# Decoder block on one core: gate columns inside the first head's value projection, keys turned by full-precision transposes, a 128-row bias product

## The chip, the cores and the metric

One core of a Trainium2 chip runs the whole block: one sequence of 1024 positions, 1024 channels, in float32. The metric is the device time of one execution in microseconds, as the median of several runs; less is better. Engines are called as in the profile: PE is TensorE, PEld its weight loads, DVE is VectorE, ACT is ScalarE, POOL is GpSimd, SP issues most DMAs.

## What is computed

```python
h = rms_norm(x, norm_mix_g) * (1.0 + sc1) + sh1
proj = h @ w_in + b_in
glu_in, qk_in, v, o_pre, if_pre, merge_pre = jnp.split(proj, IN_SPLITS, axis=-1)
...
qk = silu(causal_depthwise_conv(qk_in, qk_conv_w, qk_conv_b))
q, k = jnp.split(qk, 2, axis=-1)
...
gates = jnp.moveaxis(if_pre, -1, 1)
hm = mlstm_chunkwise(heads(q), heads(k) * (MLSTM_HEAD_DIM ** -0.5), heads(v),
                     gates[:, :MLSTM_HEADS], gates[:, MLSTM_HEADS:])
```

There are 4 heads of 256 channels. `if_pre` is 8 columns wide: an input gate and a forget gate for each head. In the recurrence the state is updated by `C = decay * C + sum_s w_s k_s v_s^T`, in which `w` comes from the gates. A convolution branch (31 taps, on the GLU of the first 2048 columns of `proj`), merge gates, an output projection and a SwiGLU FFN stand around it.

## The kernel before

Every large product is made in three parts for accuracy: each operand is split into a rounded part (hi) and the rest (lo), both in the type fp32r, and hi*hi, hi*lo and lo*hi are summed in PSUM. `hh` and `hl` hold h in that way, channels on the partitions, 8 tiles of 128 x 1024. `load_split` (L143) loads weights of 8 x 128 rows and 128 columns, ACT rounds them into `whi`, DVE subtracts to `wlo`. `wblock` (L370) makes one 128-column block of `proj` from them, 48 products of 512 columns at L159.

The stretch from about 70 to 830 us is the mixers. After two GLU tiles (`glu`, L394), the loop at L730 takes the heads in turn. For each head `qkv` (L516) makes two key tiles and two query tiles (`qk_tile`, L496: `wblock`, a 4-tap convolution on DVE, Silu on ACT, the split), then the values: `v_weights` loads 1024 x 256 weights in two halves, and `v_half` (L543) takes four tiles of 128 positions each: one bias product with `ones_v` (64 rows, two of them not zero: the bias's hi and lo at rows 0 and 32; L549), and 24 products of 256 columns (L552 to L554). ACT and DVE empty the sum into `vh` and `vl` (L559, L560).

For the first head `gates` (L412) runs in between: a generator whose steps `mix` (L383) interleaves with those of `qkv`. It loads the 8 gate columns into `wif_raw`, puts hi and lo beside each other into the first 16 of 128 weight columns (`wif`, the rest zero), makes 32 products of 512 columns (L423), copies the 16 x 1024 result to SBUF and turns it back by eight transposes with 16 rows (L432). Then come a chain of short DVE instructions, scans along the sequence, and the tables `iw`, `wsc`, `en`, `dec`, `Mc`.

`mlstm` (L593) works in four chunks of 256 positions. For three of them the keys must be turned to have positions on the partitions: L621 multiplies the key's hi and lo by `shift_id`, an identity beside zeros, four products of 256 columns for each 128 positions. The result is scaled by `wsc` into `kwh`, `kwl` (L624, L625). `mlstm` is mixed with filler blocks (GLU tiles, merge gates, output gates).

The convolution taps (L340, DVE, 128 x 1024 each) go through a list `bg`: `pump` (L82) emits some after each block with a later priority. The order on each engine is not the order of the code: a scheduler places every instruction by priority and by its own model of time. Each engine then works in that order and waits on semaphores. Buffers matter around the change: weights have two each of `wraw`, `whi`, `wlo`; the tag `t4` has three of 128 x 1024 (the sigmoids of the GLU tiles use them); PSUM has two accumulators `mm` of two banks.

Of the kernel before, what the change touches and what calls it, by code (L numbers as in the profile page):

```python
# [17 lines left out]
KT = 8  # L18
# [31 lines left out]
def hybrid_block(ctx: ExitStack, tc: tile.TileContext, x, c, w_ada, b_ada, norm_mix_g, w_in, b_in,  # L50
# [49 lines left out]
    ones_v = const.tile([64, 128], F32R, name="ones_v")  # L100
# [223 lines left out]
    shift_id = hp.tile([128, 2, 256], F32R, name="shift_id")  # L324
    nc.gpsimd.memset(shift_id.bitcast(F32), 0.0)
    nc.vector.tensor_copy(shift_id[:, 0, 0:128], ident)
    nc.vector.tensor_copy(shift_id[:, 1, 128:256], ident)
# [83 lines left out]

    def gates():  # L412
        wif_raw = hp.tile([128, KT, 8], F32, name="wif_raw")
        nc.sync.dma_start(wif_raw, win[:, IF0:IF0 + 8].rearrange("(k p) e -> p k e", p=128))
        wif = wp.tile([128, KT, 128], F32R, name="wif", tag="whi")
        nc.gpsimd.memset(wif.bitcast(F32), 0.0)
        nc.vector.tensor_copy(wif[:, :, 0:8], wif_raw)
        nc.vector.tensor_sub(wif[:, :, 8:16], wif_raw, wif[:, :, 0:8].bitcast(F32))
        acc = ps_mm()
        for k in range(KT):  # L420
            for i, rhs in enumerate((hh, hl)):
                for h in range(2):
                    nc.tensor.matmul(acc[:, h, :], wif[:, k, :], rhs[k][:, h * 512:(h + 1) * 512],  # L423
                                     start=(k == 0 and i == 0), stop=(k == KT - 1 and i == 1))
        ifT = tmp4()
        nc.scalar.activation(ifT, flat(acc), AF.Copy)
        yield

        yield
        pg = ps_a()  # L430
        for b in range(8):
            nc.tensor.transpose(pg[:, b * 16:(b + 1) * 16], ifT[0:16, b * 128:(b + 1) * 128], ident[0:16, 0:16])  # L432
        pgv = pg[:, 0:128].rearrange("p (b j) -> p b j", j=16)
        gsum = hp.tile([128, 8, 8], F32, name="gsum")
        nc.vector.tensor_add(gsum, pgv[:, :, 0:8], bif[:, None, :].to_broadcast([128, 8, 8]))
        nc.vector.tensor_add(gsum, gsum, pgv[:, :, 8:16])
# [56 lines left out]
        for t, sgn in ((iw, 1.0), (wsc, 1.0), (en, -1.0), (dec, 1.0)):  # L493
            nc.scalar.activation(t, t, AF.Exp, scale=sgn)

    def qk_tile(col0, conv_i, scale, name):  # L496
# [9 lines left out]
        nc.scalar.activation(cv, cv, AF.Silu, bias=cols["qk_b"][:, conv_i:conv_i + 1])  # L506
# [3 lines left out]
        if scale == 1.0:  # L510
            nc.vector.tensor_sub(lo, cv, hi.bitcast(F32))
        else:
            nc.vector.scalar_tensor_tensor(lo, cv, scale, hi.bitcast(F32), op0=OP.mult, op1=OP.subtract)
        return hi, lo

    def qkv(h):  # L516
# [7 lines left out]
        b_raw, b_hi, b_two = (hp.tile([64, 256], dt, name=n) for n, dt in (("vb_raw", F32), ("vb_hi", F32R), ("vb_two", F32R)))  # L524
        nc.gpsimd.memset(b_raw, 0.0)
        for r in (0, 32):
            nc.sync.dma_start(b_raw[r:r + 1, :], b_in[0:1, bcols])
# [4 lines left out]
        def v_weights():  # L532
            ws = []
            for kh in range(2):
                raw, hi, lo = (wp.tile([128, KT, 128], dt, name=n, tag=n).rearrange("p (k a) e -> p k (a e)", a=2)
                               for n, dt in (("wraw", F32), ("whi", F32R), ("wlo", F32R)))
                nc.sync.dma_start(raw, win[kh * 512:(kh + 1) * 512, bcols].rearrange("(k p) e -> p k e", p=128))
                nc.scalar.activation(hi, raw, AF.Copy)
                nc.vector.tensor_sub(lo, raw, hi.bitcast(F32))
                ws.append((hi, lo))  # L540
            return ws
# [735 lines left out]
```

## Time and profile before

| | us |
|---|---|
| median of 3 runs | 1760.76 (1760.38 to 1761.39) |
| span of the profiled execution, first to last instruction | 1757.5 |
| PE busy | 1716.9 (98%) |
| DVE busy | 1253.3 (71%) |
| ACT busy | 610.9 (35%) |
| POOL busy | 72.9 (4%) |

The time of a run and the span of the profiled execution differ by what lies around the first and the last instruction. Busy time is the time in which at least one instruction of the engine is under way; PE's products overlap, so a group's mean duration is longer than the distance from one start to the next.

### The profile page before, as it was taken

To read this page: it belongs to the slowest core of one execution; us is meant where nothing else is said; L and a number is where in the kernel's file an instruction comes from. 1 tells how busy PE (TensorE), PEld (TensorE's weight loads), DVE (VectorE), ACT (ScalarE), POOL (GpSimd) and SP (SyncE) were. 2 spreads that over 40 slices of the span, in tenths; PEclk is the share of its full clock that TensorE was granted. 3 is DMA by queue.
4 is the path that set the end of the run, shared out by engine and by line. 5 is a ranking of instruction groups with operands and counts; after the bars stand their busy time and mean duration, and the time that the engine had idled before them with its cause. 6 is when DMAs were issued, how large, how long until landed. Compare 5 with 4: busy or idle time off the path is not lost.

```text
span 1757.5 us, 21022 instructions
## 1 busy us (share of the span) xinstructions
PE 1716.9 (98%) x8448; PEld 1436.9 (82%) x8448; DVE 1253.3 (71%) x1652; ACT 610.9 (35%) x791; POOL 72.9 (4%) x121
## 2 busy tenths in 40 slices
PE   5999999999999999999999999999999999999998
PEld 4788888888888888888888788888888888878887
DVE  6888998996689858737689567866666665685243
ACT  6434334322533243223522366423222321232122
POOL 3100001000100000000000000000000000000000
PEclk8999999999999999999999999999999999999999
DMA  9121111111111211224497643322222222653221
GB/s 333 33 60 40 46 60 49 49 60 60 49 37 60 62 46 48 73 60 163 136 374 261 204 156 109 108 84 72 84 84 84 72 85 90 221 168 104 64 89 56
DMA packets 194712, 179.93 MB, mean 102 GB/s; under 512 B 7463, under 2 KB 166711, under 8 KB 194615
## 3 DMA queue, kind: packets, MB, share of 16 engines
q1 hardware_dynamic: 177367, 146.61, 26.8%
q10 hardware_dynamic: 17248, 31.99, 5.0%
q8 instruction: 66, 1.08, 0.3%
q14 instruction: 31, 0.25, 0.0%
HBM read 146.06 MB, written 32.51 MB: 102 GB/s over the span
## 4 chain that ended last, share of the span: by engine, by line
PE 90%; DVE 4%; DMA 3%; issue 1%; ACT 1%; POOL 0%; SPq 0%; POOLq 0%; DVEq 0%; ACTq 0%
PE mm L159 39%; PE mm L1054 5%; PE mm L1055 5%; PE mm L1056 4%; PE mm L552 2%; PE mm L1240 2%; PE mm L1239 2%; PE mm L1241 2%; PE mm L553 2%; PE mm L554 2%; PE pc L1054 1%; DVE macc L268 1%; PE pc L1056 1%; PE pc L1055 1%; PE pa L1056 1%
## 5 line engine op out<-in xcount | busy, mean ns | idle before, releaser
L340 DVE SCALAR_TENSOR_TENSOR cacc<-a,col,cacc 128x1024 f32<-128x1024 f32 x240 | 307.3, 1286 | 4.1 <-ACT cacc L338 1.4
L159 PE MATMUL mm<-hh,whi 128*128 128x512 f32 x864 | 272.8, 392 | 0.8 <-ACT t L364 0.8
L159 PE MATMUL mm<-hl,whi 128*128 128x512 f32 x864 | 271.0, 392 | 0.0
L159 PE MATMUL mm<-hh,wlo 128*128 128x512 f32 x864 | 270.6, 391 | 0.0
L159 PEld LDWEIGHTS mm<-hh,whi 128*128 128x128 f32 x864 | 161.1, 188 | 32.8 <-ACT t L364 1.2
L159 PEld LDWEIGHTS mm<-hh,wlo 128*128 128x128 f32 x864 | 161.3, 188 | 32.3
L159 PEld LDWEIGHTS mm<-hl,whi 128*128 128x128 f32 x864 | 160.5, 188 | 30.9 <-issue 0.2
L149 ACT ACTIVATE whi<-wraw 128x1024 fp32r<-128x1024 f32 x62 | 65.8, 1062 | 228.7 <-PE mm L159 178.5
L150 DVE TENSOR_TENSOR wlo<-wraw,whi 128x1024 fp32r<-128x1024 f32 x60 | 73.2, 1220 | 26.1 <-ACT whi L149 26.0
L552 PE MATMUL mm<-whi,hh 128*128 128x256 f32 x256 | 76.2, 298 | 0.0
L1054 PE MATMUL mm<-Bh,gh 128*128 128x512 f32 (+1 forms) x192 | 71.6, 375 | 1.5 <-ACT gh L994 1.0
L553 PE MATMUL mm<-whi,hl 128*128 128x256 f32 x256 | 72.5, 283 | 0.0
L1055 PE MATMUL mm<-Bl,gh 128*128 128x512 f32 (+1 forms) x192 | 71.5, 373 | 0.6 <-DVE Bl L976 0.6
L554 PE MATMUL mm<-wlo,hh 128*128 128x256 f32 x256 | 71.8, 283 | 0.0
L1056 PE MATMUL mm<-Bh,gl 128*128 128x512 f32 (+1 forms) x192 | 71.2, 372 | 0.0
L505 DVE SCALAR_TENSOR_TENSOR cacc<-qkraw,col,cacc 128x1024 f32<-128x1024 f32 x48 | 61.5, 1280 | 6.7 <-ACT cacc L503 6.0
L1243 DVE TENSOR_TENSOR x<-x,mm 128x1024 f32<-128x1024 f32 x24 | 29.3, 1219 | 51.1 <-PE mm L1241 47.0
L1119 ACT ACTIVATE whi<-wraw 128x512 fp32r<-128x512 f32 (+2 forms) x32 | 25.3, 790 | 110.6 <-PE mm L1241 72.9
L552 PEld LDWEIGHTS mm<-whi,hh 128*128 128x128 f32 x256 | 48.8, 191 | 4.1
L1240 PE MATMUL mm<-fa,wlo 128*128 128x512 f32 x128 | 50.1, 392 | 1.0 <-DVE wlo L1120 0.9
L1239 PE MATMUL mm<-fa,whi 128*128 128x512 f32 x128 | 50.0, 390 | 0.9 <-DVE cu L1082 0.9
L1241 PE MATMUL mm<-fa,whi 128*128 128x512 f32 x128 | 49.9, 390 | 0.0
(442 smaller groups left out, 3898.0 us busy)
## 6 DMA issues: line engine op xcount, KB each, us to landing
wraw<-in_w_in_dram SPq DMA_DIRECT2D x64, 512.0 KB, 4.2
awt<-in_w_ada_dram SPq DMA_DIRECT2D x32, 512.0 KB, 8.1
graw<-in_w_ffn_up_dram SPq DMA_DIRECT2D x24, 512.0 KB, 3.8
uraw<-in_w_ffn_up_dram SPq DMA_DIRECT2D x22, 512.0 KB, 4.7
draw<-in_w_ffn_down_dram SPq DMA_DIRECT2D x22, 512.0 KB, 4.4
act_d<-cg ACTq DMA_DIRECT2D x38, 256.0 KB, 2.2
wad<-in_w_ada_dram SPq DMA_DIRECT2D x16, 512.0 KB, 10.2
wraw<-in_w_out_dram SPq DMA_DIRECT2D x16, 512.0 KB, 4.3
```

Of the source, the lines that this page charges most:

```text
L150: (eng or nc.vector).tensor_sub(lo, raw, hi.bitcast(F32))
L159: nc.tensor.matmul(flat(acc)[:, a:b], lhs[:, k, :], rhs[k][:, a:b], start=(first and k == 0), stop=(last and k == kt - 1))
L340: nc.vector.scalar_tensor_tensor(acc, a[:, j:j + S], dw_col(j, ct), acc, op0=OP.mult, op1=OP.add)
L552: nc.tensor.matmul(o, hh[k][:, ts_], hi[:, k % 4, :], start=False, stop=False)
L553: nc.tensor.matmul(o, hl[k][:, ts_], hi[:, k % 4, :], start=False, stop=False)
L554: nc.tensor.matmul(o, hh[k][:, ts_], lo[:, k % 4, :], start=False, stop=(k == KT - 1))
L1054: nc.tensor.matmul(o, a, rh, start=(k == 0), stop=False)
L1055: nc.tensor.matmul(o, a, rl, start=False, stop=False)
L1056: nc.tensor.matmul(o, b, rh, start=False, stop=(k == 3))
L1239: nc.tensor.matmul(o, hi[:, i, :], his[i][:, a:b], start=(i == 0), stop=False)
L1240: nc.tensor.matmul(o, lo[:, i, :], his[i][:, a:b], start=False, stop=False)
L1241: nc.tensor.matmul(o, hi[:, i, :], los[i][:, a:b], start=False, stop=(i == nf - 1))
```

## The change

It has three parts. The gate columns no longer have products of their own: in the first head's value projection the rounded weights get 16 more columns (8 hi, 8 lo), and DVE sums them out of PSUM into `gsum`. For that the wide weights (272 columns a row tile) lie in the three `t4` buffers, an accumulator holds two tiles of positions in place of four, and the values of each head are a generator of their own (`v_part`), which runs ahead of keys and queries for the first head and behind them for the others. The bias product has 128 rows, with more zeros. And the keys are turned by transposes of a full-precision copy `kf` (the first 768 positions, the three chunks that need it); the factor 1/16 of the keys goes into `wsc`.

```diff
-    ones_v = const.tile([64, 128], F32R, name="ones_v")
+    ones_v = const.tile([128, 128], F32R, name="ones_v")
...
-    shift_id = hp.tile([128, 2, 256], F32R, name="shift_id")
-    nc.gpsimd.memset(shift_id.bitcast(F32), 0.0)
-    nc.vector.tensor_copy(shift_id[:, 0, 0:128], ident)
-    nc.vector.tensor_copy(shift_id[:, 1, 128:256], ident)
...
+    gsum = hp.tile([128, 8, 8], F32, name="gsum")
+    wif_raw = hp.tile([128, KT, 8], F32, name="wif_raw")
+    nc.sync.dma_start(wif_raw, win[:, IF0:IF0 + 8].rearrange("(k p) e -> p k e", p=128))
+
     def gates():
-        wif = wp.tile([128, KT, 128], F32R, name="wif", tag="whi")
...
-        nc.vector.tensor_copy(wif[:, :, 0:8], wif_raw)
-        nc.vector.tensor_sub(wif[:, :, 8:16], wif_raw, wif[:, :, 0:8].bitcast(F32))
-        acc = ps_mm()
-        for k in range(KT):
-            for i, rhs in enumerate((hh, hl)):
-                for h in range(2):
-                    nc.tensor.matmul(acc[:, h, :], wif[:, k, :], rhs[k][:, h * 512:(h + 1) * 512],
-                                     start=(k == 0 and i == 0), stop=(k == KT - 1 and i == 1))
-        ifT = tmp4()
-        nc.scalar.activation(ifT, flat(acc), AF.Copy)
...
-        pg = ps_a()
-        for b in range(8):
-            nc.tensor.transpose(pg[:, b * 16:(b + 1) * 16], ifT[0:16, b * 128:(b + 1) * 128], ident[0:16, 0:16])
...
-        nc.vector.tensor_add(gsum, pgv[:, :, 0:8], bif[:, None, :].to_broadcast([128, 8, 8]))
-        nc.vector.tensor_add(gsum, gsum, pgv[:, :, 8:16])
         gview = gsum.rearrange("p (c s) j -> p s c j", s=2)
         nc.vector.tensor_copy(gi, gview[:, :, :, 0:4])
...
             nc.scalar.activation(t, t, AF.Exp, scale=sgn)
+        nc.vector.tensor_scalar(wsc, wsc, 1.0 / 16, None, op0=OP.mult)
...
-        nc.scalar.activation(cv, cv, AF.Silu, bias=cols["qk_b"][:, conv_i:conv_i + 1])
+        bias = cols["qk_b"][:, conv_i:conv_i + 1]
+        if name == "k":
+            kf = hp.tile([128, 768], F32, name=f"kf{conv_i % 2}")
+            nc.scalar.activation(kf, cv[:, 0:768], AF.Silu, bias=bias)
+            nc.scalar.activation(cv[:, 768:S], cv[:, 768:S], AF.Silu, bias=bias)
+            hi, lo = (hp.tile([128, S], F32R, name="k" + n, tag="k" + n, bufs=2) for n in "hl")
+            for src, a, b in ((kf, 0, 768), (cv[:, 768:S], 768, S)):
+                nc.scalar.activation(hi[:, a:b], src, AF.Copy, scale=scale)
+                nc.vector.scalar_tensor_tensor(lo[:, a:b], src, scale, hi[:, a:b].bitcast(F32), op0=OP.mult, op1=OP.subtract)
+            return hi, lo, kf
+        nc.scalar.activation(cv, cv, AF.Silu, bias=bias)
...
-    def qkv(h):
+    def v_part(h):
...
-        b_raw, b_hi, b_two = (hp.tile([64, 256], dt, name=n) for n, dt in (("vb_raw", F32), ("vb_hi", F32R), ("vb_two", F32R)))
+        b_raw, b_hi, b_two = (hp.tile([128, 272], dt, name=n) for n, dt in (("vb_raw", F32), ("vb_hi", F32R), ("vb_two", F32R)))
...
+        his, los = [], []
+        if h == 0:
+            wide = [ha.tile([128, S], F32R, name="t4", tag="t4", bufs=3)[:, 0:816].rearrange("p (k e) -> p k e", e=272) for _ in range(3)]
+            his = [wide[k // 3][:, k % 3] for k in range(KT)]
+            for i, t in enumerate(wide):
+                n = min(3, KT - 3 * i)
+                ks = slice(3 * i, 3 * i + n)
+                nc.vector.tensor_copy(t[:, 0:n, 256:264], wif_raw[:, ks])
+                nc.vector.tensor_sub(t[:, 0:n, 264:272], wif_raw[:, ks], t[:, 0:n, 256:264].bitcast(F32))
+        for kh in range(2):
+            raw, hi, lo = (wp.tile([128, KT, 128], dt, name=n, tag=n).rearrange("p (k a) e -> p k (a e)", a=2)
+                           if n != "whi" or h else None for n, dt in (("wraw", F32), ("whi", F32R), ("wlo", F32R)))
+            nc.sync.dma_start(raw, win[kh * 512:(kh + 1) * 512, bcols].rearrange("(k p) e -> p k e", p=128))
...
+                his += [hi[:, k] for k in range(4)]
+            else:
+                for t, a, k0, k1 in (((wide[0], 0, 0, 3), (wide[1], 0, 3, 4)), ((wide[1], 1, 0, 2), (wide[2], 0, 2, 4)))[kh]:
+                    o = t[:, a:a + k1 - k0, 0:256]
+                    nc.scalar.activation(o, raw[:, k0:k1], AF.Copy)
+                    nc.vector.tensor_sub(lo[:, k0:k1], raw[:, k0:k1], o.bitcast(F32))
+            los += [lo[:, k] for k in range(4)]
...
+        for g in range(8 // n):
             acc = ps_mm()
-            for i in range(4):
-                t = g * 4 + i
+            for i in range(n):
+                t = g * n + i
...
-                o = acc[:, i // 2, (i % 2) * 256:(i % 2) * 256 + 256]
-                nc.tensor.matmul(o, ones_v, b_two, start=True, stop=False)
+                o = acc[:, i // 2, (i % 2) * 256:(i % 2) * 256 + 256] if h else acc[:, i, 0:272]
+                nc.tensor.matmul(o, ones_v, b_two[:, 0:w], start=True, stop=False)
                 for k in range(KT):
-                    hi, lo = ws[k // 4]
-                    nc.tensor.matmul(o, hh[k][:, ts_], hi[:, k % 4, :], start=False, stop=False)
-                    nc.tensor.matmul(o, hl[k][:, ts_], hi[:, k % 4, :], start=False, stop=False)
-                    nc.tensor.matmul(o, hh[k][:, ts_], lo[:, k % 4, :], start=False, stop=(k == KT - 1))
+                    nc.tensor.matmul(o, hh[k][:, ts_], his[k], start=False, stop=False)
+                    nc.tensor.matmul(o[:, 0:256], hh[k][:, ts_], los[k], start=False, stop=False)
+                    nc.tensor.matmul(o, hl[k][:, ts_], his[k], start=False, stop=(k == KT - 1))
                 pump(PUMP / 4)
                 yield
...
-
+            if h == 0:
+                gs = gsum[:, 2 * g:2 * g + 2]
+                nc.vector.tensor_add(gs, acc[:, :, 256:264], bif[:, None, :].to_broadcast([128, 2, 8]))
+                nc.vector.tensor_add(gs, gs, acc[:, :, 264:272])
+        return vh, vl
+
+    def qk_part(h):
         q, k = [], []
...
-        ws = v_weights()
-        for g in range(2):
-            yield from v_half(g, ws)
-        return q, k, vh, vl
+        return q, k
...
                     for j in range(2):
-                        for i in range(2):
-                            nc.tensor.matmul(o, k[j][i][:, ks], shift_id[:, j, :], start=(j == 0 and i == 0),
-                                             stop=(j == 1 and i == 1))
+                        nc.tensor.transpose(o[:, j * 128:(j + 1) * 128], k[j][2][:, ks], ident)
                     w = wsc[:, s, c, h:h + 1]
...
         if h == 0:
-            qkv0 = returned(qkv(0), box)
-            mix(gates(), qkv0, GM)
-            run(qkv0)
+            qk0 = returned(qk_part(0), box)
+            run(returned(v_part(0), vbox))
+            mix(gates(), qk0, GM)
+            run(qk0)
         else:
-            run(returned(qkv(h), box))
+            run(returned(qk_part(h), box))
+            run(returned(v_part(h), vbox))
```

The scheduler orders the instructions anew. On PE, the place behind the second GLU tile (`mm` is the accumulator in PSUM, `whi`, `wlo` the weights, `hh`, `hl` the block's input) read before:

```order
L159 MATMUL mm_635<-hl7_460,whi_631 128x512 x2
L159 MATMUL mm_635<-hh7_89,wlo_632 128x512 x2
L423 MATMUL mm_707<-hh0_82,wif_703 128x512 x2
L423 MATMUL mm_707<-hl0_314,wif_703 128x512 x2
L423 MATMUL mm_707<-hh1_83,wif_703 128x512 x2
L423 MATMUL mm_707<-hl1_317,wif_703 128x512 x2
```

Now the value projection of the first head stands there, and takes its first four products of the first accumulator and of the second before it comes to the weights in the third buffer (`t4_716`):

```order
L551 MATMUL mm_794<-wlo_731,hh4_86 128x256
L552 MATMUL mm_794<-t4_715,hl4_407 128x272
L550 MATMUL mm_794<-t4_715,hh5_87 128x272
L551 MATMUL mm_794<-wlo_731,hh5_87 128x256
L552 MATMUL mm_794<-t4_715,hl5_410 128x272
L550 MATMUL mm_737<-t4_716,hh6_88 128x272
L551 MATMUL mm_737<-wlo_731,hh6_88 128x256
L552 MATMUL mm_737<-t4_716,hl6_457 128x272
```

The 32 products of L423 are gone, and 38 products stand between the GLU tile and the first one that reads `t4_716`.

On DVE, at the same place (`a` is the second GLU tile's product, `cacc` the conv taps, `wlo` the low part of the v weights, `gsum` the gate sums):

```order
L341 SCALAR_TENSOR_TENSOR a_685<-mm_631,col5_513,t4_625 128x1024
L537 TENSOR_TENSOR wlo_731<-wraw_730,t4_715 128x512
L336 SCALAR_TENSOR_TENSOR cacc_577<-a_563,col3_517,cacc_577 128x1024
L523 CAST t4_716<-wif_raw_698 128x2x8
L537 TENSOR_TENSOR wlo_731<-wraw_730,t4_716 128x512
L336 SCALAR_TENSOR_TENSOR cacc_577<-a_563,col3_517,cacc_577 128x1024
L524 TENSOR_TENSOR t4_716<-wif_raw_698,t4_716 128x2x8
L336 SCALAR_TENSOR_TENSOR cacc_577<-a_563,col4_521,cacc_577 128x1024 x4
L558 TENSOR_TENSOR vl_701<-mm_737,vh_700 128x2x256
L561 TENSOR_TENSOR gsum_697<-mm_737,bif_403 128x16
L336 SCALAR_TENSOR_TENSOR cacc_577<-a_563,col4_521,cacc_577 128x1024
L562 TENSOR_TENSOR gsum_697<-gsum_697,mm_737 128x16
```

Before, `a` was followed by one low part of a key's weights and then by taps; now the split of the third weight tile and the emptying of the accumulators stand between the taps.

In the first chunk of the first head, PE's list around the turned keys (`pa`, `pn` are PSUM, `vh`, `sch` the values and the scores) changes in this way:

```order
-L621 MATMUL pa_1440<-shift_id_537,kh_838 128x256
-L621 MATMUL pa_1440<-shift_id_537,kl_839 128x256
-L621 MATMUL pa_1440<-shift_id_537,kh_939 128x256
-L621 MATMUL pa_1440<-shift_id_537,kl_940 128x256
-L573 MATMUL pn_1469<-vh_742,sch_1427 128x258
+L621 MATMUL pa_1420<-ident_69,kf0_1063 128x128
+L621 MATMUL pa_1420<-ident_69,kf1_1178 128x128
+L574 MATMUL pn_1445<-vh_700,sch_1407 128x258
```

Four products become two transposes, at the same place between the filler's products and the first product with the scores; there are 24 such places.

## Rows read from the trace of the kernel before

**Rows 1.** The page, busy time, share of the span and instructions of each engine.
```profile
PE 1716.9 (98%) x8448; PEld 1436.9 (82%) x8448; DVE 1253.3 (71%) x1652; ACT 610.9 (35%) x791; POOL 72.9 (4%) x121
```

**Rows 2.** Busy time by stretch: length, then each engine, clock, DMA share, GB/s.
```profile
core 0: us, PE busy (x) PEld busy (x) DVE busy (x) ACT busy (x) POOL busy (x), PEclk, DMA share, GB/s
90.00:140.00 50.00, 50.00 (x228) 41.13 (x227) 44.97 (x61) 19.49 (x20) 0.42 (x4) 1.00 0.22 64
...
170.00:330.00 160.00, 160.00 (x883) 138.12 (x882) 144.53 (x180) 57.67 (x70) 12.70 (x22) 1.00 0.19 53
...
650.00:830.00 180.00, 180.00 (x968) 154.26 (x967) 118.73 (x161) 56.06 (x68) 6.40 (x13) 1.00 0.26 82
990.00:1000.00 10.00, 6.46 (x22) 4.93 (x21) 7.31 (x10) 3.69 (x4) 0.00 (x0) 0.83 0.63 197
```

**Rows 3.** Timeline of PE around a bias product: start, duration, line, operands, count.
```profile
148.12 0.28 PE L554 MATMUL mm<-wlo,hh 128*128 128x256 f32 x1
148.32 0.38 PE L549 MATMUL mm<-vb_two,ones_v 64*128 64x256 f32 x1
148.63 0.39 PE L552 MATMUL mm<-whi,hh 128*128 128x256 f32 x1
148.86 0.28 PE L553 MATMUL mm<-whi,hl 128*128 128x256 f32 x1
```

**Rows 4.** Groups of PE by form: count, busy time, mean duration.
```profile
L621 PE MATMUL pa<-shift_id,kh 128*128 128x256 f32 x48 | 12.4, 280 | 0.0
L549 PE MATMUL mm<-vb_two,ones_v 64*128 64x256 f32 x32 | 12.2, 380 | 0.0
```

**Rows 5.** Timeline of PE around the gates' eight small transposes.
```profile
104.74 0.61 PE L159 MATMUL mm<-hh,wlo 128*128 128x512 f32 x2
105.29 0.67 PE L432 MATMUL pa<-ident,t 16*128 16x16 f32 x8
105.89 0.74 PE L159 MATMUL mm<-hh,whi 128*128 128x512 f32 x2
106.47 0.63 PE L159 MATMUL mm<-hl,whi 128*128 128x512 f32 x2
```

**Rows 6.** Timeline of PE, first of the gates' products and first one after them.
```profile
89.78 0.62 PE L423 MATMUL mm<-hh,wif 128*128 128x512 f32 x2
...
97.04 0.62 PE L159 MATMUL mm<-hh,whi 128*128 128x512 f32 x2
```

**Rows 7.** Timeline of PE around one group of turned keys.
```profile
202.31 0.28 PE L621 MATMUL pa<-shift_id,kh 128*128 128x256 f32 x1
...
202.79 0.28 PE L573 MATMUL pn<-vh,sch 128*128 128x258 f32 x1
202.91 0.28 PE L574 MATMUL pn<-vl,sch 128*128 128x258 f32 x1
```

**Rows 8.** Timeline of PE around two transposes of the decay mask.
```profile
175.36 0.62 PE L159 MATMUL mm<-hh,whi 128*128 128x512 f32 x2
175.82 0.38 PE L582 MATMUL pa<-ident,Mc 128*128 128x128 f32 x2
...
176.50 0.62 PE L159 MATMUL mm<-hh,wlo 128*128 128x512 f32 x2
```

**Rows 9.** The page, DMA issues: count, KB each, median us to landing.
```profile
wraw<-in_w_in_dram SPq DMA_DIRECT2D x64, 512.0 KB, 4.2
```

**Rows 10.** Timeline of DVE before and at the end of the second GLU tile.
```profile
80.09 0.19 DVE L417 CAST wif<-wif_raw 128x64 fp32r<-128x64 f32 x1
...
81.55 7.88 DVE L340 SCALAR_TENSOR_TENSOR cacc<-a,col,cacc 128x1024 f32<-128x1024 f32 x6
90.05 1.28 DVE L345 SCALAR_TENSOR_TENSOR a<-mm,col,t 128x1024 f32<-128x1024 f32 x1 [0.62 <-PE mm L159]
91.25 1.22 DVE L150 TENSOR_TENSOR wlo<-wraw,whi 128x1024 fp32r<-128x1024 f32 x1
```

**Rows 11.** Waits of PE: what was waited for, in total, times, longest.
```profile
PE pa L946 <- ACT whi L940: 3.5, 1, 3.5
```

More of the change, by code (lines that the diff above doesn't have):

```diff
@@ L509, in qk_tile @@
         nc.scalar.activation(hi, cv, AF.Copy, scale=scale)
[L510 to L513, printed above, removed]
+        nc.vector.tensor_sub(lo, cv, hi.bitcast(F32))
         return hi, lo
-    def qkv(h):
+    def v_part(h):
         vh = hp.tile([128, 8, 258], F32R, name="vh")
@@ L523, in qkv @@
         bcols = slice(V0 + h * 256, V0 + h * 256 + 256)
-        b_raw, b_hi, b_two = (hp.tile([64, 256], dt, name=n) for n, dt in (("vb_raw", F32), ("vb_hi", F32R), ("vb_two", F32R)))
+        b_raw, b_hi, b_two = (hp.tile([128, 272], dt, name=n) for n, dt in (("vb_raw", F32), ("vb_hi", F32R), ("vb_two", F32R)))
         nc.gpsimd.memset(b_raw, 0.0)
         for r in (0, 32):
-            nc.sync.dma_start(b_raw[r:r + 1, :], b_in[0:1, bcols])
+            nc.sync.dma_start(b_raw[r:r + 1, 0:256], b_in[0:1, bcols])
         nc.scalar.activation(b_hi, b_raw, AF.Copy)
@@ L530, in qkv @@
         nc.vector.tensor_sub(b_two[32:64, :], b_raw[32:64, :], b_hi[32:64, :].bitcast(F32))
[L532 to L537, printed above, removed]
+        his, los = [], []
@@ L538, in v_weights @@
+        for kh in range(2):
+            raw, hi, lo = (wp.tile([128, KT, 128], dt, name=n, tag=n).rearrange("p (k a) e -> p k (a e)", a=2)
+                           if n != "whi" or h else None for n, dt in (("wraw", F32), ("whi", F32R), ("wlo", F32R)))
+            nc.sync.dma_start(raw, win[kh * 512:(kh + 1) * 512, bcols].rearrange("(k p) e -> p k e", p=128))
+            if h:
                 nc.scalar.activation(hi, raw, AF.Copy)
                 nc.vector.tensor_sub(lo, raw, hi.bitcast(F32))
-                ws.append((hi, lo))
@@ L544, in v_half @@
+        n = 4 if h else 2
+        w = 256 if h else 272
+        for g in range(8 // n):
             acc = ps_mm()
-            for i in range(4):
-                t = g * 4 + i
+            for i in range(n):
+                t = g * n + i
                 ts_ = slice(t * 128, (t + 1) * 128)
-                o = acc[:, i // 2, (i % 2) * 256:(i % 2) * 256 + 256]
-                nc.tensor.matmul(o, ones_v, b_two, start=True, stop=False)
+                o = acc[:, i // 2, (i % 2) * 256:(i % 2) * 256 + 256] if h else acc[:, i, 0:272]
+                nc.tensor.matmul(o, ones_v, b_two[:, 0:w], start=True, stop=False)
@@ L555, in v_half @@
+                    nc.tensor.matmul(o, hl[k][:, ts_], his[k], start=False, stop=(k == KT - 1))
                 pump(PUMP / 4)
                 yield
-            pv = acc.rearrange("p a (b e) -> p (a b) e", b=2)
-            dst = (slice(None), slice(g * 4, g * 4 + 4), slice(0, 256))
+            pv = acc.rearrange("p a (b e) -> p (a b) e", b=2) if h else acc[:, :, 0:256]
+            dst = (slice(None), slice(g * n, g * n + n), slice(0, 256))
             nc.scalar.activation(vh[dst], pv, AF.Copy)
@@ L731, in hybrid_block @@
         box = []
+        vbox = []
         if h == 0:
-            qkv0 = returned(qkv(0), box)
-            mix(gates(), qkv0, GM)
-            run(qkv0)
-        else:
-            run(returned(qkv(h), box))
+            qk0 = returned(qk_part(0), box)
+            run(returned(v_part(0), vbox))
+            mix(gates(), qk0, GM)
+            run(qk0)
+        else:
+            run(returned(qk_part(h), box))
+            run(returned(v_part(h), vbox))
         dms = decay_mask(h)
@@ L742, in hybrid_block @@
             next(fill, None)
-        mix(mlstm(h, hm, *box[0], dms), fill, STEPS[h])
+        mix(mlstm(h, hm, *box[0], *vbox[0], dms), fill, STEPS[h])
         run(fill)
```

9 lines of the change are left out of this document (removed).

## The prediction

> **What bounds the kernel.** I read the page's busy line first: PE is at work in 98% of the span, DVE in 71% [rows 1]. Then the stretches: in every one that the change touches PE is busy all the time (50.00 of 50, 160.00 of 160) at the full granted clock, while DVE is close behind, at 44.97 of 50 and 144.53 of 160 [rows 2]. So between 90 and 830 us a PE instruction that goes away shortens the end by its own slot, as long as DVE does not become the limit there. The reader should look at start-to-start distances in the timeline, not at durations: a 256-column product has a duration of 0.28 but the next one starts 0.12 later [rows 3]. The busy times of the groups hide what an instruction costs the queue, and all terms below are slots.
>
> **Part 1, bias product with 128 rows instead of 64** (32 instructions [rows 4], the same number after). From the last product before one to the product two after it takes 148.86 - 148.12 = 0.74 us [rows 3]. Two of the three slots in it are ordinary ones of 0.12, so the bias product takes 0.50: 0.08 is lost before it, 0.19 in its own slot, 0.11 after it. With 128 rows I price it as its neighbours, which have the same 256 columns and 128 rows: 0.12. Gain 32 x 0.38 = **12.1 us**. Bounds: 0, if the loss has to do with being the bias or the first of a sum, and 12.1. I take the upper one because the loss appears a second time where only the row count is special: around the eight 16-row transposes of the gates the same 0.10 before (104.74 + 0.45 to 105.29) and 0.13 after (105.89 to 106.47 instead of 0.45) are lost [rows 5], and because the first products of the gates' sum start on the beat [rows 6].
> [...]
>
> **Part 2, gate columns.** Removed: 32 products of 512 columns, 97.04 - 89.78 = 7.26 us [rows 6], and the eight small transposes, which cost 106.47 - 104.74 = 1.73 less two ordinary pairs of 0.45, so 0.82 [rows 5]. Added: 16 columns on 2 x 8 x 8 = 128 value products and on 8 bias products. From 256 columns (0.12 [rows 3]) to 512 (7.26 / 32 = 0.227 [rows 6]) a column costs 0.42 ns, so 16 cost 7 ns, and 136 of them 0.9 us; a step at 256 is not to be seen, since a 258-column product takes 0.12 as well [rows 7]. Bounds of the added part: 0, and 136 x 0.107 = 14.6 us if 272 columns ran like 512. I take 0.9, by the nearest row, 258. Net gain 7.26 + 0.82 - 0.9 = **7.2 us**.
> Off PE the edit drops a memset on POOL and one ACT copy, and adds on DVE six short splits of gate columns and eight short sums. They lie under PE (part 4).
>
> **Part 3, keys by transposes.** Removed: 24 groups of four 256-column products (96 instructions, half of which are the group in [rows 4]), 202.79 - 202.31 = 0.48 each [rows 7]. Added: 24 pairs of full-precision 128 x 128 transposes. The nearest row has just this form: a pair for the decay mask stands between products, and from 175.36 to 176.50 there are two pairs of products (0.45 each) and the transposes, so the pair costs 0.23 [rows 8]. Gain 24 x 0.25 = **5.9 us** (unrounded 0.486 less 0.24). Bounds for a pair: 0.23, and 2 x 0.27 = 0.54, if transposes did not overlap at all; I take 0.24. [...]
> The key tile now runs Silu and the split in two pieces: per key tile two more instructions on ACT and one on DVE, eight times. They hide under PE; without cover they would cost at most a DVE pass of 1.3 us each, 10 us.
>
> **Part 4, what the new order makes late.** v_part(0) now follows the second GLU tile directly, where the gates used to give DVE 7.3 us to prepare. Its two loads take the place of the first key tiles' loads in SP's queue, issued long before, so they wait for nothing new; the key tiles' loads now follow once the v weights are split, need about 4.2 us each [rows 9], and have v_part's 25 us to land in. The eight gate columns' load keeps its place behind the two weight loads. The third weight tile can be filled only when DVE has read the second GLU gate out of the third t4 buffer. I walk DVE through its new queue: the GLU product from 90.05 to 91.3, low part of k 4 and 5 (half of 1.22) to 91.9, a conv tap (7.88 / 6 = 1.31) to 93.2, the cast 0.2 to 93.4, low part of k 6 and 7 to 94.0, a tap to 95.3, the last split 0.2 to 95.5 [rows 10]. PE has 38 products ordered ahead of the first that needs that tile, 4.65 us from 89.8, so it arrives at 94.45 and waits **1.1 us**. After that each accumulator of two tiles (6.2 us of products) is emptied by DVE in one tap, 0.6 for the low part and two short sums, twice buffered: no wait. Bounds: 0, and 1.1 + 4 x 1.31 = 6.3 if each of the four emptyings comes one tap too late. The gate chain starts about 27 us later than before, but its transposes are ordered within the second key tile and the first query tile, and the decay masks after the fourth; by the same walk DVE has each input some 3 us before PE asks for it. The vector load over the whole stretch grows by few us, and PE's shrinks by 25 of some 740, so DVE rises from 90% to about 94% in its fullest stretch: close, not over.
>
> **Sum.** 12.1 + 7.2 + 5.9 - 1.1 = 24.1 us. The profiled execution's span is 1757.5; 1757.5 - 24.1 = 1733.4. The median of the runs is 1760.76, 3.3 us above that span, which the change does not touch: **1736.7 us**, 1.4% less.
>
> **The rivals.**
> (a) The bias product keeps its loss, because what costs is the first product of a sum whose weights are a constant, and not the row change. Then 1736.7 + 12.1 = 1748.8. Against it stands the 16-row group [rows 5]. [...] 5%.
> (b) One of the two new product forms costs its upper bound: transposes that do not overlap give 1736.7 + 24 x 0.30 = 1744; 272 columns at the price of 512 give 1736.7 + 13.7 = 1750.4. For it: no row shows 272. Against it: 258 columns and the decay-mask pair. 6% in all, two thirds of that for the first. [...]
> (c) DVE comes late in v_part(0) and again in the first head's mixing, each emptying by a tap or two: 3 to 9 us, so 1740 to 1746. For it: DVE at 90% in order, with 1.3 us taps between the short instructions that PE waits for. Against it: PE has a second accumulator and waits nowhere there today. 14%.
> (d) Slower than before: the waits in v_part(0) repeat until the granted clock falls. After the one long wait of the second half (3.5 us [rows 11]) the stretch around it shows 0.83 of full clock [rows 2]. [...] It decides if each of the four waits is like that one of 3.5 us; I get 1.1 once. 3%.
> That the change does not do what it says is excluded for the counts: on PE's list the 32, 8 and 96 are gone and the 136 and 48 are there.
>
> **Numbers.** Forecast, 1733.5 to 1740: 72%. With (c) and the transposes of (b) 90% of the chance lies between 1733.5 and 1746; I stop at 1745, which leaves out (a), the 272 columns, (d) and the worst of (c), under 2 in 10. About 0.2%, 3.5 us, can be told from no change; all cases but (d) are faster than that, and I leave 2% for a surprise near zero: faster 0.95, same 0.02, slower 0.03.
>
> **What would show it.** In the profile after: bias products 0.12 after their neighbours and none at 0.50; no 512-column gate products; value products of head 0 about 0.127 apart; two transposes of the keys in 0.23 to 0.24; PE's waits between 85 and 120 us of about 1 us in sum; PE still at 100% from 120 to 800. It is wrong if bias products still cost 0.3 or more, if PE waits for gsum or vl by more than 3 us, or if the clock leaves 1.00 there.

## The result and the profile after

The changed kernel takes **1746.48 us** (median of 4 runs, 1746.38 to 1747.80), the kernel before 1760.57 (4 runs, 1759.94 to 1761.39). The ratio is 0.9921, with a 95% interval of 0.9907 to 0.9935. It is faster by 14.1 us; the forecast was 24.1 us, and 1746.48 lies above the range, which ends at 1745.

The page of the profile after, busy line, which answers to [rows 1], and the windows that answer to [rows 2] (length, PE, PEld, DVE, ACT, POOL, granted clock, DMA share, GB/s):

```profile
PE 1694.8 (97%) x8360; PEld 1420.3 (81%) x8360; DVE 1253.1 (72%) x1673; ACT 612.9 (35%) x811; POOL 66.0 (4%) x119
```

```profile
90.00:140.00 50.00, 49.45 (x312) 44.79 (x310) 43.42 (x72) 15.57 (x21) 0.60 (x3) 1.00 0.19 53
170.00:330.00 160.00, 157.45 (x877) 136.41 (x876) 147.74 (x183) 63.86 (x78) 9.93 (x23) 1.00 0.18 50
650.00:830.00 180.00, 180.00 (x954) 154.23 (x953) 117.13 (x160) 56.32 (x68) 7.94 (x13) 1.00 0.29 91
985.00:995.00 10.00, 9.04 (x28) 7.25 (x29) 7.44 (x10) 5.31 (x10) 0.00 (x0) 0.67 0.62 184
```

In the stretch of 160 us PE was never idle before and now is for 2.55 us. The last row lies in the output projection, right behind a wait of 8 us: PE's granted clock there is 0.67.

Did the three parts do what they should? The bias product of another head (timeline of PE), beside [rows 3], is now on the beat of its neighbours, as the starts show: 0.11 to 0.12 from each one to the next.

```profile
285.76 0.28 PE L552 MATMUL mm<-whi,hl 128*128 128x256 f32 x1
285.87 0.28 PE L548 MATMUL mm<-vb_two,ones_v 128*128 128x256 f32 x1
285.99 0.28 PE L550 MATMUL mm<-whi,hh 128*128 128x256 f32 x1
286.11 0.28 PE L551 MATMUL mm<-wlo,hh 128*128 128x256 f32 x1
```

Two transposes of the keys, in place of the four products of [rows 7]. From 202.38 to 202.95 there are, beside them, one product of 512 columns (0.23) and one of 258 (0.12), so the pair costs 0.22:

```profile
202.38 0.39 PE L159 MATMUL mm<-hh,whi 128*128 128x512 f32 x1
202.61 0.38 PE L621 MATMUL pa<-ident,kf 128*128 128x128 f32 x2
202.74 0.37 PE L574 MATMUL pn<-vh,sch 128*128 128x258 f32 x1
202.95 0.28 PE L575 MATMUL pn<-vl,sch 128*128 128x258 f32 x1
```

So these two prices hold. The waits of PE from 70 to 1000 us (what was waited for, total, times, longest), beside [rows 11], which before was the only one above 1 us in this stretch:

```profile
PE pa L948 <- ACT whi L942: 7.8, 1, 7.8
PE pc L576 <- DVE kwl L624: 1.8, 1, 1.8
PE mm L159 <- DVE wlo L150: 1.2, 2, 0.7
PE mm L550 <- DVE t L524: 0.6, 1, 0.6
PE pc L574 <- ACT kwh L623: 0.3, 1, 0.3
```

Where the time went is read best from the **lead**: the same product is looked up in both traces, and its start after is subtracted from its start before.

| product | start before, us | lead, us |
|---|---|---|
| first of the second GLU tile | 67.88 | -0.42 |
| one behind the last head's mixing | 836.30 | 19.96 |
| first of the output projection | 970.44 | 19.97 |
| 145th of the output projection | 1008.78 | 14.62 |
| first of the FFN | 1068.06 | 13.95 |
| last of the FFN's down projection | 1751.09 | 12.88 |

The change earned 20.0 us in the mixers instead of 24.1, and then 5.35 us were lost within 40 us at the start of the output projection, a place that the diff does not touch. In the output projection the long wait is the mark of it: 3.70 us before, 7.97 after (from one start to the next, beyond the usual distance). It stands ahead of the stage's 97th product before, and of the 121st after.

What stands behind that wait? ACT's timeline (line numbers are each kernel's own), of the kernel before and then of the changed one. `whi` splits the output projection's weights, `s3h` and `Th` are the split of an FFN block that is made ahead and parked (`up_park`, with `up_sums`, L1000), `mm<-x` empties the first sums of the output projection.

```profile
973.60 0.37 ACT L885 ACTIVATE mrow<-pa 8x256 f32<-8x256 f32 x1 [2.32 <-PE pa L884]
...
983.52 1.06 ACT L940 ACTIVATE whi<-wraw 128x1024 fp32r<-128x1024 f32 x1 [5.85 <-DMA x<-in_x_dram]
993.38 0.63 ACT L994 ACTIVATE s3h<-s 128x512 fp32r<-128x512 f32 x1 [8.79 <-DVE s L1003]
994.11 1.06 ACT L994 ACTIVATE Th<-uraw 128x1024 fp32r<-128x1024 f32 x1
995.07 1.04 ACT L940 ACTIVATE whi<-wraw 128x1024 fp32r<-128x1024 f32 x1
997.11 1.06 ACT L994 ACTIVATE Th<-graw 128x1024 fp32r<-128x1024 f32 x1 [1.00 <-DVE graw L1006]
```

```profile
957.97 0.38 ACT L887 ACTIVATE mrow<-pa 8x256 f32<-8x256 f32 x1 [0.36 <-PE pa L886]
...
967.09 1.06 ACT L942 ACTIVATE whi<-wraw 128x1024 fp32r<-128x1024 f32 x1 [3.10 <-PE mm L949]
977.98 0.63 ACT L996 ACTIVATE s3h<-s 128x512 fp32r<-128x512 f32 x1 [9.83 <-DVE s L1005]
979.17 1.06 ACT L996 ACTIVATE Th<-uraw 128x1024 fp32r<-128x1024 f32 x1 [0.57 <-DVE uraw L1006]
980.14 0.58 ACT L956 ACTIVATE mm<-x 128x512 f32<-128x512 f32 x1
...
983.91 1.06 ACT L996 ACTIVATE Th<-graw 128x1024 fp32r<-128x1024 f32 x1 [3.07 <-DVE graw L1008]
984.87 1.04 ACT L942 ACTIVATE whi<-wraw 128x1024 fp32r<-128x1024 f32 x1
```

The order is another one. Before, the weight split that PE waited for stood behind one `Th`; now it stands behind both and an emptying between them. From `s3h` to that split it is 1.69 us before and 6.89 after. DVE's order is part of it: 3.07 of the 6.89 are ACT's wait for `graw`, whose last sum on DVE (L1008, at 983.20) now stands behind four emptying steps of the output projection (L954 and L955, from 977.86 on); before, none stood between these sums. And what all of them wait for, the parked block's load `uraw`, is issued late relative to PE, as SP's rows show, before and after:

```profile
974.00 0.64 SPq L887 DMA_DIRECT2D mrow_d<-mrow  x2
...
977.41 0.53 SPq L990 DMA_DIRECT2D uraw<-in_w_ffn_up_dram  x1
```

```profile
958.37 0.64 SPq L889 DMA_DIRECT2D mrow_d<-mrow  x2
959.12 0.39 SPq L941 DMA_DIRECT2D wraw<-in_w_out_dram  x1
...
962.32 1.16 SPq L992 DMA_DIRECT2D uraw<-in_w_ffn_up_dram  x1
```

`uraw` is issued 15.1 us earlier, though PE is 20.0 us earlier: it is queued behind the store of `mrow`, which ACT now makes after the last splits of `y` and another weight split (before, ahead of them), and behind one more load of weights. DVE begins to use it 15.2 us after its issue before, 14.9 after.

### The profile page after: what moved, and what is told of

Its sections match the earlier page's. It is cut to its first block, busy times and chain, and to the rows that moved or that the text cites. A ratio compares the mean times of both kernels' runs of the same rounds, so it can differ in the third digit from the quotient of the medians.

```text
span 1744.6 us, 20880 instructions
## 1 busy us (share of the span) xinstructions
PE 1694.8 (97%) x8360; PEld 1420.3 (81%) x8360; DVE 1253.1 (72%) x1673; ACT 612.9 (35%) x811; POOL 66.0 (4%) x119
## 4 chain that ended last, share of the span: by engine, by line
PE 88%; DVE 6%; DMA 3%; issue 2%; ACT 1%; POOL 0%; SPq 0%; ACTq 0%; POOLq 0%; DVEq 0%
PE mm L159 39%; PE mm L1056 5%; PE mm L1057 5%; PE mm L1058 4%; PE mm L1242 2%; PE mm L1243 2%; PE mm L1241 2%; PE mm L550 1%; PE mm L552 1%; PE mm L551 1%; PE pc L1056 1%; PE pc L1058 1%; PE pc L1057 1%; PE pa L1058 1%; PE pa L1057 1%
## 5 line engine op out<-in xcount | busy, mean ns | idle before, releaser
L150 DVE TENSOR_TENSOR wlo<-wraw,whi 128x1024 fp32r<-128x1024 f32 x60 | 73.0, 1217 | 22.2 <-ACT whi L149 18.8
L482 DVE SCALAR_TENSOR_TENSOR cacc<-qkraw,col,cacc 128x1024 f32<-128x1024 f32 x48 | 61.5, 1281 | 5.3 <-ACT cacc L480 4.6
L550 PE MATMUL mm<-whi,hh 128*128 128x256 f32 x192 | 54.4, 283 | 0.0
L552 PE MATMUL mm<-whi,hl 128*128 128x256 f32 x192 | 54.2, 283 | 0.0
L997 DVE TENSOR_TENSOR ul<-uraw,uh 128x1024 fp32r<-128x1024 f32 x20 | 24.5, 1224 | 35.5 <-ACT uh L996 35.5
```

Source lines behind the costliest of these rows:

```text
L150: (eng or nc.vector).tensor_sub(lo, raw, hi.bitcast(F32))
L550: nc.tensor.matmul(o, hh[k][:, ts_], his[k], start=False, stop=False)
L552: nc.tensor.matmul(o, hl[k][:, ts_], his[k], start=False, stop=(k == KT - 1))
```

## The experiments

Two theories for the loss at the output projection. **Order theory:** the changed program places ACT's, DVE's and SP's instructions there in another order, and that order costs it. **Load theory:** PE comes 20 us earlier, but the loads that burst there do not, so that any gain in the mixers is partly given back. The kernels beside the kernel before, with the lead at three of the products above, of the profiled executions. A lead compares two single executions. In the mixers it repeats well (e4, whose mixers are untouched, has -0.03; the changed kernel, e3, e5 and e11 have 19.93 to 20.06). But runs of one kernel differ by some us (the kernel before: 1758.82 to 1763.48), and where in a run that arises no trace shows, so a difference of 1 or 2 us behind the mixers can be that.

| kernel | run, us | ratio to before, 95% | end of mixers | 145th product | last product |
|---|---|---|---|---|---|
| changed | 1746.48 | 0.9921, 0.9907 to 0.9935 | 19.96 | 14.62 | 12.88 |
| e1 bias part alone | 1748.02 | 0.9932, 0.9917 to 0.9947 | 12.19 | 12.18 | 11.92 |
| e2 keys alone | 1761.29 | 1.0005, 0.9995 to 1.0014 | 5.35 | 0.68 | -1.39 |
| e3 changed, parked blocks on POOL | 1740.06 | 0.9886, 0.9871 to 0.9901 | 20.06 | 23.87 | 20.57 |
| e4 before, parked blocks on POOL | 1759.91 | 0.9997, 0.9988 to 1.0006 | -0.03 | 1.10 | 0.05 |
| e5 changed, PUMP 5800 | 1743.81 | 0.9906, 0.9889 to 0.9922 | 19.93 | 19.22 | 16.00 |
| e6 gate columns alone | 1757.31 | 0.9982, 0.9973 to 0.9991 | 5.63 | 3.67 | 1.22 |
| e7 changed, keys undone | 1747.77 | 0.9934, 0.9920 to 0.9949 | 15.43 | 14.35 | 12.67 |
| e8 changed, PUMP 4400 | 1783.16 | 1.0132, 1.0117 to 1.0147 | -21.36 | -21.99 | -23.56 |
| e9 before, 96-row bias | 1748.70 | 0.9936, 0.9919 to 0.9953 | 11.82 | 11.86 | 12.16 |
| e10 keys alone, blocks on POOL | 1754.71 | 0.9967, 0.9954 to 0.9980 | 5.52 | 9.37 | 5.86 |
| e11 changed, first block on POOL | 1740.35 | 0.9882, 0.9867 to 0.9897 | 20.06 | 23.64 | 18.65 |
| e12 blocks on POOL, PUMP 5800 | 1741.28 | 0.9892, 0.9877 to 0.9907 | 18.37 | 19.54 | 16.27 |

**e1, the bias part alone.**

```diff
-    ones_v = const.tile([64, 128], F32R, name="ones_v")
+    ones_v = const.tile([128, 128], F32R, name="ones_v")
...
-        b_raw, b_hi, b_two = (hp.tile([64, 256], dt, name=n) ...
+        b_raw, b_hi, b_two = (hp.tile([128, 256], dt, name=n) ...
```

> The kernel before with nothing but the 128-row bias product (ones_v and the three bias tiles get 128 rows). Slot theory: 32 x 0.38 = 12.1 us go in the mixers, less 0 to 2 us of new waits for DVE there. For the 6 us that the whole change gave back at the start of the output projection there are two theories. Order theory (the give-back comes from the order in which the split of the parked FFN block and the emptying of the sums now stand on ACT and DVE; here they stand as before): the wait before the second part of the output projection stays 3.5 to 4 us, nothing is given back, the run takes 1748.5 to 1750.5. Load theory (PE comes earlier but the burst of loads at the start of the stage does not, so the give-back grows with the lead): the wait grows to about 6 us and the run takes 1752 to 1754. [...]

12.4 us by the medians, all of it kept. ACT at the output projection, and PE's longest wait there:

```profile
971.30 1.06 ACT L940 ACTIVATE whi<-wraw 128x1024 fp32r<-128x1024 f32 x1 [5.82 <-DMA x<-in_x_dram]
981.16 0.63 ACT L994 ACTIVATE s3h<-s 128x512 fp32r<-128x512 f32 x1 [8.79 <-DVE s L1003]
...
982.85 1.04 ACT L940 ACTIVATE whi<-wraw 128x1024 fp32r<-128x1024 f32 x1
```

```profile
PE pa L946 <- ACT whi L940: 3.5, 1, 3.5
```

Every row stands 12.2 us before its row of the kernel before, loads included, and the wait is the same 3.5. Loads do come earlier when PE does: the load theory falls for this part.

**e2, the keys alone:** `kf`, the split in two pieces, the transposes and 1/16 in `wsc`, put into the kernel before.

```diff
-                        for i in range(2):
-                            nc.tensor.matmul(o, k[j][i][:, ks], shift_id[:, j, :], ...
+                        nc.tensor.transpose(o[:, j * 128:(j + 1) * 128], k[j][2][:, ks], ident)
```

> The kernel before with nothing but the keys turned by transposes (kf, Silu and split in two pieces, 1/16 in wsc). In the mixers 24 x 0.25 = 5.9 us go, less about 2.4 us if the waits for the key's low part (kwl) that the whole change shows near 277 us belong to this part. Order theory: ACT and DVE stand at the output projection as in the whole change, so 4 to 6 us are given back there although the lead is small, the wait is 7 to 8 us, and the run takes 1757 to 1762. Load theory: the give-back goes with the lead, 1 to 2 us, and the run takes 1755 to 1758.

The mixers are 5.35 us shorter, and the run is no shorter at all. The waits near 277 us are not there (the largest in the mixers is 0.68), but the order at the output projection is that of the changed kernel, and so is the wait:

```profile
992.39 0.63 ACT L996 ACTIVATE s3h<-s 128x512 fp32r<-128x512 f32 x1 [9.63 <-DVE s L1005]
993.59 1.06 ACT L996 ACTIVATE Th<-uraw 128x1024 fp32r<-128x1024 f32 x1 [0.57 <-DVE uraw L1006]
...
999.29 1.04 ACT L942 ACTIVATE whi<-wraw 128x1024 fp32r<-128x1024 f32 x1
```

```profile
PE pa L948 <- ACT whi L942: 7.6, 1, 7.6
```

A lead of 5 us loses 4.7 there, one of 20 loses 5.35. With e1 this decides for the order, which came with the keys. In every kernel here with the old order the long wait stands ahead of the 97th product, and where no other edit touches the parked blocks it is 3.3 to 4.1 us by PE's list of waits (the kernel before, e1, e5 to e9); with the new order it stands ahead of the 121st and is 7.6 and 7.8 (e2 and the changed kernel).

**e3 and e4, the parked blocks on POOL,** in the changed kernel and in the one before: the four sums and three splits of `up_park`.

```diff
-        nc.vector.tensor_sub(s3, g[:, 0:4], u[:, 0:4])
+        nc.gpsimd.tensor_sub(s3, g[:, 0:4], u[:, 0:4])
...
-            split_into(*spare(kp), wide(t))
+            nc.gpsimd.tensor_copy(a, t)
+            nc.gpsimd.tensor_sub(b, t, a.bitcast(F32))
```

> The changed kernel, with the sums and splits of the two parked FFN blocks (up_park) on POOL in place of DVE and ACT, so that no split of the output projection's weights stands behind them. If ACT and DVE, waiting in order for the parked block's load, are what holds the weight split: the 8.0 us wait falls to 2 us or less, the clock stays up behind it, and the run takes 1738 to 1741. If the weights of the output projection themselves land too late in the burst of loads: the wait stays above 5 us and the run takes 1743 to 1747.

> The kernel before, with the same edit as in the run before this one (parked FFN blocks on POOL). If waiting in order for the parked block's load is what holds PE: the 3.7 us wait and the 2 us of lower clock behind it go, 1755 to 1757. If it is the weights' own load: 1759 to 1761. The distance between this kernel and the changed one with the same edit is the value of the change without the give-back: 19 to 20 us expected.

e3 is 6.4 us faster than the changed kernel, by the medians, and beats both kernels. PE's waits at the output projection:

```profile
PE pc L1064 <- ACT sh L1047: 2.4, 1, 2.4
PE pa L948 <- ACT whi L942: 1.3, 1, 1.3
```

7.8 became 1.3, so most of it was waiting behind the parked block, and not the weights' own load; the 1.3 that is left is that load (ACT stands idle for 0.60 us until `wraw` lands, and then makes the split). SP's order is still the new one in e3 (`uraw` is issued at 961.93), so at this wait its late issue costs PE nothing by itself: what costs is that the weight split stands behind the block's steps on ACT and DVE. How much is ACT's order and how much DVE's was not tried apart. The 2.4 is a new wait at the end of that stage. e4 missed its 1755 to 1757: its wait only fell from 3.5 to 2.4 and the gain of 1.1 was gone by the end. With the same edit on both sides the change is worth 1759.91 - 1740.06 = 19.9 us, what it earned in the mixers. That the two agree so closely is partly chance: from e4 to e3 the lead is 20.1 in the mixers, 22.8 at the 145th product, 18.8 at the first of the FFN and 20.5 at the end.

**e5, the old order by another way:** all three parts, `PUMP` changed.

```diff
-PUMP = 5500
+PUMP = 5800
```

> The changed kernel with PUMP 5800 in place of 5500, a slightly larger allowance of conv taps behind each block. All three parts stay. In the program's order the start of the output projection stands again as it did before the change on ACT (y splits, weight split, s3h, Th, weight split, Th, then the emptying of the sums) and on SP (the gate row ahead of the next weight load). Order theory: the long wait is 3.5 to 4 us again, nothing of the lead is given back, the run takes 1739 to 1742 if the mixers stay as they are. If it is not the order but the earlier arrival: a wait near 8 us and 1745 to 1747.

```profile
974.17 0.63 ACT L996 ACTIVATE s3h<-s 128x512 fp32r<-128x512 f32 x1 [8.80 <-DVE s L1005]
974.90 1.06 ACT L996 ACTIVATE Th<-uraw 128x1024 fp32r<-128x1024 f32 x1
975.86 1.04 ACT L942 ACTIVATE whi<-wraw 128x1024 fp32r<-128x1024 f32 x1
```

```profile
PE pa L948 <- ACT whi L942: 3.6, 1, 3.6
```

Mixers and waits in them are as in the changed kernel, the split stands behind one `Th`, the wait is 3.6, and of the 19.9 us 19.2 are left at the 145th product (14.6 in the changed kernel). The run is slower than expected, 1743.8: some 2 us more are lost in the down projection, in two waits of 1.4 and 1.5 for weight splits there. Why those grew was not tried.

**e6 and e7, the gate columns alone, and the changed kernel without the keys' part.** e6 is the changed kernel with 64 bias rows and the shift products, e7 has only the latter back (the reverse of the lines under e2).

> The changed kernel without two of its parts: the bias product has 64 rows again and the keys are turned by shift products again, so that the gate columns are what is left. By the slots 7.26 + 0.82 - 0.9 = 7.2 us go in the mixers, less 0.7 us for the wait at the third wide weight tile. ACT and SP stand at the output projection as before the change. Order theory: nothing is given back, 1753 to 1755. Load theory: 1755 to 1757.

> The changed kernel with the shift products back, the other two parts as changed. Order theory: 12.1 + 7.2 less some 2 us of waits for DVE, 17 to 19 us, all of it kept at the output projection, where the order is the old one: 1741 to 1744, faster than with the third part. If the parts simply add up: 1746.5 + 5.4 = 1752. In the mixers the 2.4 us of waits for kwh and kwl near 277 us go if they come from the third part, and stay if they come from DVE's taps in a shorter stretch.

e6 is 2.3 us above what the order theory gave it, and next to the load theory's 1755 to 1757: in the mixers 5.63 us, with waits of 0.49 and 0.71 for ACT and DVE, then 2.0 us lost at the output projection (its wait is 4.28) and 2.4 after it, though the order on ACT is the old one. e7 loses 1.1 us at the output projection instead of 5.35, as the order theory says, but its run of 1747.8 misses the 1741 to 1744: its mixers gain 15.4 and not 17 to 19, with a wait of 1.79 at 308 us, and another 1.7 us go behind the 145th product. It is no faster than the changed kernel; by simple adding it would have taken 1752. So the old order does not keep everything: in e1, e5, e6, e7 and e9 0 to 2 us go there even so, and from there to the end between nothing and 3.2 us. At the output projection that is small against the 4.7 and 5.35 us of the new order (e2 and the changed kernel). From the mixers to the end it is not: up to 4.4 us (e6) against 6.7 and 7.1. What sets it stays open.

**e8, fewer taps in the mixers:** `PUMP` 4400.

> The changed kernel with PUMP 4400 in place of 5500: one conv tap less behind each block, so less of DVE's work between the mixers' products, and more of it left for the end of the mixers. If the 3.9 us of new waits in the mixers (277, 309, 488 us) come from taps ahead of the short instructions on DVE: they fall below 1.5 us and the lead after the last block of the mixers grows from 20.0 to 22 us or more, unless the taps that are left over stop PE at the layer norm. If they come from ACT's pieces of the keys: they stay. The order at the output projection is the old one: wait 3.5 to 4 us by the order theory, run 1738 to 1742.

A miss. The taps that were left over stop PE at the layer norm:

```profile
PE pn L779 <- DVE t4b L773: 30.9, 1, 30.9
```

And the mixers' waits did not fall: the two near 277 us are gone, but 0.45 at 282, 2.16 at 307, 0.92 at 487 and 0.80 at 667 us stand there, 5.1 us in sum with that at 95 us, against 4.6 in the changed kernel. Fewer taps alone don't buy the short instructions an earlier place. At the output projection the order is the old one, and the wait is 3.3, near the 3.5 to 4 expected.

**e9, 96 rows** (the lines of e1 with 96).

> The kernel before with a 96-row bias product: ones_v and the three bias tiles get 96 rows in place of 64. If any other number of rows than the neighbours' 128 costs the 0.38 us: nothing changes, 1759 to 1761. If 64 rows are another arrangement of the array for the chip and 96 rows are not: the bias products cost 0.12 us each and the run takes 1748 to 1749, as with 128 rows. If the loss goes with the number of rows left out: in between, 1754.

```profile
290.54 0.28 PE L553 MATMUL mm<-whi,hl 128*128 128x256 f32 x1
290.66 0.28 PE L549 MATMUL mm<-vb_two,ones_v 96*128 96x256 f32 x1
290.78 0.28 PE L552 MATMUL mm<-whi,hh 128*128 128x256 f32 x1
```

The whole 12 us again. The price is not one of rows left out, nor of a row count unlike the neighbours'; 64 rows have it (0.50 us in all, [rows 3]) and 96 do not (0.12). Whether 64 rows are another arrangement of the array, as the second case supposes, no run here shows.

**e10, the keys alone, with the parked blocks on POOL** (the edits of e2 and e3).

> The kernel before with the keys' transposes alone and the parked FFN blocks on POOL. Order theory: the 5.35 us that this part gained in the mixers and lost again at the output projection stay, the wait there is under 2.6 us, and the run takes 1753.5 to 1756.5, against 1759.9 for the kernel before with the parked blocks on POOL. If the loss behind the mixers has another cause (the lead is lost wherever the loads burst): 1758.5 to 1760.5.

With the wait out of the way (1.1 us), the keys' part is worth 1759.91 - 1754.71 = 5.2 us, what it earns in the mixers. Without that edit it was worth nothing.

**e11 and e12, two tries for more:** POOL for the first parked block only (the edit of e3 under `if f == 0`), and the edits of e3 and e5 together.

> The changed kernel with the sums and splits of only the first parked block on POOL; the second stays on DVE and ACT. With both on POOL a new wait of 2.4 us stood at the end of the output projection (the second block's sums reach PE late). If that wait came from the second block on POOL: the 8 us wait stays at 1.5 us, the wait of 2.4 us goes and the run takes 1737 to 1739. If the second block, back on ACT, holds a later weight split: 1739 to 1743.

> Both edits that helped: parked blocks on POOL, and PUMP 5800. The first takes the parked blocks out of ACT's and DVE's order, the second restores the old order of the rest. If their gains at the output projection are of one and the same wait, nothing is added: 1739 to 1742. If the old order also spares the 2.4 us wait at the end of the output projection: 1736 to 1738.

Neither is told from e3; the times are those of e11's second case and e12's first. In e11 the wait of 2.4 at the end is gone, and one of 2.5 at an emptying (PE for `pc` of L956) has come; in e12 the wait at the start is 2.7 instead of 1.3.

## Why the prediction was wrong

**The slots were right.** In the mixers the sum of PE's start-to-start times fell from 768.42 to 748.04, by 20.4 us, and 4.6 us of it after are new waits: 25.0 us of slots, against 12.1 + 7.2 + 5.9 = 25.2 forecast. (The 0.12 for a 256-column product, which part 1 reads from [rows 3], stands in [rows 7].) Each part alone, with the waits in it and the start of the mixers set right:

- Bias, part 1: 12.19 - 0.16 = 12.0 (12.1 forecast), and rival (a) is out. The product costs 0.50 us with 64 rows [rows 3] and 0.12 with 128 and with 96 (the changed kernel and e9), so 64 rows lose 0.38 and 96 lose nothing. What the 0.38 is, no trace here shows.
- Gate columns, part 2: 5.63 + 0.11 + 1.2 = 6.9 (7.2).
- Keys, part 3: 5.35 + 0.08 + 0.68 = 6.1 (5.9); the pair cost 0.22. Both cases of rival (b) are out: 272 columns take 0.12 to 0.13 from start to start (94.25 to 94.74 us in the changed kernel). A transpose lasts 0.27 by its duration (the median of the 48 of L621), more than the 0.22 that the pair costs PE, and the granted clock was 1.00 from 170 to 830 us, where all of them lie.

**Part 4 was too small by 3.5 us.** The wait at the third wide weight tile is there, 0.72 instead of 1.1. But the walk through DVE's queue stopped with the first head, by the sentence that DVE "has each input some 3 us before PE asks for it". Later, PE waits 0.47 and 1.93 near 277 us, 0.60 at 309 and 0.91 at 488 (from one start to the next, beyond the usual distance, so a little more than PE's list of waits has). These are waits of the kind that rival (c) described, the first two in the first head's last turned keys, the others behind that head, and none at an emptying of the values. The rows of DVE at 277:

```profile
275.94 1.22 DVE L531 TENSOR_TENSOR wlo<-wraw,whi 128x1024 fp32r<-128x1024 f32 x1
277.07 0.41 DVE L645 TENSOR_TENSOR num<-num,pn 128x258 f32<-128x258 f32 x1
277.40 1.28 DVE L482 SCALAR_TENSOR_TENSOR cacc<-qkraw,col,cacc 128x1024 f32<-128x1024 f32 x1
278.60 0.48 DVE L624 SCALAR_TENSOR_TENSOR kwl<-pa,wsc,kwh 128x256 fp32r<-128x256 f32 x1
```

The key's high part was ready at 276.6, yet `kwl` (0.48) came after a tap of 1.28; that tap is one of the next key's own 4-tap convolution (L482), which `PUMP` does not ration. At 488 two taps stand between the bias split and `wlo`, where before there was one. Each part alone had 0.0 (e1), 0.7 (e2) and 1.2 us (e6) of such waits, the whole 4.6: DVE's share of 92% in this stretch is not over, but PE's cover for its order is gone. That the parts' gains don't add up (12.19 + 5.63 + 5.35 = 23.2, together 19.96) is shown; that moving those taps would give it back was not tried. That rival (d) would be slower than before was the author's estimate: nothing here shows `v_part(0)` at a lowered clock, which in the changed kernel was 1.00 from 90 to 140 us.

**The step that failed is the Sum,** and under it the sentence that a PE instruction that goes away in the mixers "shortens the end by its own slot". It subtracts what is earned up to 830 us from the end of the program, as if the order behind 830 us were the one of before. It was not: the keys' part made the placing come out otherwise at the output projection, 5.35 us were lost there (4.3 by the longer wait, and 1.0 by products at the lower granted clock behind it, 0.50 in both kernels: 0.43 us apart instead of 0.23, 13 of them instead of 8), and 1.7 more up to the end. No rival named it. [Rows 11] had a wait of 3.5 us behind the same parked block, and I used it as a price for rival (d) only. The question that it asked was which instructions stand ahead of that weight split on ACT, and whether they stand so in the changed program; the program's order would have shown it.

The outcome 1746.48 lies next to the end of rival (c)'s band, 1746, but not by its mechanism alone: of the 9.8 us that are missing 3.5 are of that kind, 0.2 were too much in the slots, 7.1 went behind the mixers and 0.4 ahead of them, and 1.4 came back by luck. The Sum took the 3.3 us from the profiled span to the median as fixed, and after it is 1.9. Every run stands 1.7 to 2.2 us above its own span; the rest of such a distance (it goes from -0.2 to 3.4 in the other kernels) is how the one profiled execution lies among the runs. That of the kernel before lies some 1.5 us under its median: other runs of that kernel with its span, 1757.5, took 1759.23 and 1759.26.

## What to carry to other kernels

Where a program places every instruction by its own model of time, a local edit can reorder a stage hundreds of microseconds later: take each long wait in the trace of before, and compare what stands ahead of the waited-for instruction on its engine in both programs. Price the earned slots where they are earned, but follow the lead of a few fixed products through to the end; a part whose slots all came true (the keys, 5.35 us) was worth nothing until a queue more than 200 us behind its last transposes was cleared. When work that waits for a late load sits in order on ACT or DVE ahead of work that PE needs, try an idle engine for it: POOL was worth 6.4 us here, against 2.7 for the old order by way of `PUMP` (e5). It is not a gain everywhere: in the kernel before, the same edit was worth nothing that can be told.

## What was not expected of the hardware

A 96-row product among 128-row ones runs on their beat of 0.12 us (e9), as one with 128 rows does (0.12 in the changed kernel), while one with 64 rows takes 0.50 in all [rows 3]. And a pair of full-precision 128 x 128 transposes takes 0.22 us of PE's time in the profile after, less than two products of 256 columns (0.24) and less than the duration of one of the two (0.27), at a granted clock of 1.00.
